# Projection pairs of a two-block layer: a wider allowance for VectorE's side tasks, another order of the projections around the pooling products, and the pooling gate stored and multiplied later

## The chip, the core and the metric

The kernel runs on one core of a Trainium2 chip. The metric is device time in microseconds (us), a median over runs. The engines: PE (matmuls), DVE (VectorE), ACT (ScalarE), POOL (GpSimd) and SP, which here only issues DMAs. Each engine takes its instructions in the order in which the program wrote them, and waits at an instruction until what it needs is there.

## What is computed

Two layers, one after the other, on a sequence of 1024 positions and width 1024, in float32. The change lies in the first one, a layer with three branches:

```
proj = u @ w_in + b_in            # 96 column tiles of 128
a_v, a_g, b_b, b_c, b_h, b_g, c_a, c_b, c_g, merge = jnp.split(proj, ...)
pooled = causal_multiscale_pool(a_v)          # windows 2, 4, 8, 16, four groups
y_a = einsum("bsgi,gio->bsgo", pooled, pool_w) * pool_scale * silu(a_g)
y_b = b_b * causal_dwconv(b_c * b_h, sc_w, sc_b) * silu(b_g)
h_c = causal_dwconv(c_a * sigmoid(c_b), cf_w, cf_b)      # 31 taps
y_c = silu(layer_norm(h_c)) * silu(c_g)
m = sum over n of sigmoid(merge)[n] * (y_n @ w_branch[n])
```

Then come an output projection with a layer norm, and a second layer (attention, gating and a gated MLP).

## The kernel before

Every float32 matmul is made of three products of split operands: a number is split into a high part (a copy rounded by ACT) and a low part (the difference, by DVE); `hilo` (line 163) does it. A tile is 128 channels by 1024 positions.

**Order of the work.** `self.slots` is a list that the Python program goes through once, in `run`; it writes all instructions out. No scheduler runs on the chip: what stands earlier in an engine's list comes first.

**Projections.** The 96 column tiles of `w_in` are made in two ways. The first 30 are plain slots (`slot_u`): 48 matmuls each. Then come pairs (`pair_u`, run by `run_two`): two column tiles together in seven products of 12 matmuls (a scheme that saves one product in eight), into two of four PSUM pairs. Between the products DVE combines PSUM halves (tiles `two` and `pp`), makes weight sums (`sums`) and low parts (`w`, `A`) for this pair and the next; ACT makes the high parts and one copy out of PSUM per pair (`two`, line 451), for which the fourth product waits. The name `raw` is a pair's loaded weights.

**Side tasks of DVE.** The 31-tap convolution is 31 DVE instructions per channel tile: one at line 720 and 30 taps (`h<-p,par_t,h`). They wait in a queue, `bgq`. A plain slot takes `bg` of them. In a pair, `fill` (line 439) takes tasks as long as an account of DVE's time, `now[0]`, stays within 0.2 us of that of the products, `now[1]`; each task has a cost in the account. A pair's epilogue (its activations, stores and DVE steps) is a task list too, done in the next pair. When a convolution tile is done, ACT squares it and POOL adds it and its square to two sums (lines 735, 736).

**Pooling.** `open_a` first takes everything that is left in `bgq` and then changes the SBUF pool. For each of the groups 3, 2, 1, 0 there are then: a pair for `a_v`, a pair for `a_g`, and `pool_slot`, 24 matmuls with the small `pool_w`. The pooled sums (`s`, `v`, `cn`) and their split (`ph`, `pl`) are tasks of the `a_v` pair's epilogue, made by DVE during the `a_g` pair; `split` of the second half comes last. The tile `v` has one buffer. The gates `ag` stay in SBUF, and line 971 multiplies the pooling result by scale and gate in one DVE step before the store to `ya_sp`.

**Branch products.** `end` loads the first branch weights (`wr`) and half of `yb_sp` when the last pooling product is due; `first_y` splits that half, `open_q` loads the rest (`ld`), and `branch` runs the 24 products of the three branches, b first, then a, then c. For branch c `prep_y` normalises and multiplies before it splits.

Of the kernel before, what the change touches and what calls it, by code (L numbers as in the profile page):

```python
# [21 lines left out]
H = 512  # L22
# [83 lines left out]
class Kernel:  # L106
# [125 lines left out]
    def run(self):  # L232
# [45 lines left out]

        self.release, self.resume = release, resume
        self.dma_ahead, self.split_ahead, self.hl = dma_ahead, split_ahead, hl  # L280
# [113 lines left out]
    def run_two(self, g, n):  # L394
# [44 lines left out]
        def fill():  # L439
            while later or self.bgq:  # L440
                q = later or self.bgq
                cost = getattr(q[0], "cost", 1.3)
                if now[0] + cost > now[1] + 0.2:
                    return
                q.popleft()()
                now[0] += cost
# [259 lines left out]
    def block1(self):  # L706
# [3 lines left out]
        d = lambda n, m=NK: [self.dram.tile([P, 1024], F, name="%s%d" % (n, i)) for i in range(m)]  # L710
        h_sp, ya_sp, yb_sp, cg_sp, mg_sp, m_sp = (
            d("h_sp"), d("ya_sp"), d("yb_sp"), d("cg_sp"), d("mg_sp", 24), d("m_sp"))
        st_sp = d("st_sp", 2)
# [138 lines left out]
        for j in range(plain):  # L852
            for ct, epi in ((C_B, epi_cb), (C_A, epi_ca), (B_C, lambda j: short_conv(j)[0]),
                            (B_H, epi_bh), (B_G, lambda j: short_conv(j)[4]), (B_B, epi_bb)):
                if j or ct in (B_H, B_G, B_B):
                    self.slot_u(ct + j, epi(j), bg=5)
                    self.slots[-1].aux = 1 if j > 1 else 0
                    if self.slots[-1].aux:
                        self.slots[-1].bg = 4
        pairs = Pairs(self.pair_tiles(lambda: self.cw, 1, True), lambda: None, lambda: None)  # L860
# [5 lines left out]
        self.slots[-2].tail = lambda: self.two_begin(pairs)  # L866
        self.slots[-1].tail = begin
        self.slots.append(Slot(pre=lambda: self.open_psum(4, 0)))

# [5 lines left out]
        merge = iter(range(0, 24, 2))  # L875
        gate = iter(range(0, 8, 2))

# [23 lines left out]
        def epi_av(g):  # L901
            def one(j, ps):
                s = {}
                c = lambda: self.c1.tile([P, 1040], F, tag="s", name="s", bufs=2)

                def head():
                    v = s["v"] = s["c"] = self.c1.tile([P, 1040], F, tag="v", name="v")
                    s["w"] = 1
                    nc.gpsimd.memset(v[:, 0:16], 0.0)
                    self.act(v[:, 16:1040], ps, AF.Identity, bias=self.bias_in(A_V + j))  # L910
                    if j % 2 == 0:
                        T["pw"] = self.c1.tile([P, H], F, tag="pw", name="pw")
                        nc.sync.dma_start(T["pw"], I["pool_w"][g])

                def double():
                    cur, w = s["c"], s["w"]
                    nxt = c()
# [19 lines left out]
                n = g + 1  # L937
                return [Task(0, head)] + [Task(1.25, double)] * n + [Task(1.8, out), Task(1.25, split)]
# [7 lines left out]
        def epi_ag(g):  # L946
            def one(j, ps):
                t = self.c1.tile([P, 1040], F, tag="s", name="ag", bufs=2)
                T["ag", j] = t[:, 0:1024]
                self.act(T["ag", j], ps, AF.Silu, bias=self.bias_in(A_G + j))  # L950
            return lambda x, y: [Task(0, lambda: one(2 * g, x)), Task(0, lambda: one(2 * g + 1, y))]

        def pool_slot(g):
            s = {}

            def mm():
# [11 lines left out]
            def one(c):  # L968
                j = 2 * g + c
                e = T["ag", j]  # L970
                self.stt(e, s["ps"][c], self.par("pool_scale", j), e, ALU.mult, ALU.mult)
                nc.sync.dma_start(ya_sp[j], e)

            def epi():
                pairs.todo = [Task(1.3, lambda: one(0)), Task(1.3, lambda: one(1))]
                if g == 0:
                    first_y()
                    pairs.flush()

            self.slots.append(Slot([], mm, epi, pre=pairs.flush, name="pool%d" % g))  # L980

        def open_a():
# [5 lines left out]
            self.ca = ExitStack()  # L988
            self.c1 = self.ca.enter_context(self.pool("ca", reuse_waits="tile"))

        self.slots.append(Slot(pre=open_a))
        for g in (3, 2, 1, 0):
            pair_u(A_V + 2 * g, A_V + 2 * g + 1, epi_av(g))
            pair_u(A_G + 2 * g, A_G + 2 * g + 1, epi_ag(g))
            pool_slot(g)

        def end():
# [4 lines left out]
            for j in range(4):  # L1002
# [4 lines left out]
                nc.sync.dma_start(T["ld"][1, j], yb_sp[j])  # L1007

        def last_pool():
            pairs.flush()  # L1010
            end()
            self.split_ahead(1)

        self.slots[-1].pre = last_pool

# [13 lines left out]
        def load_y(n, j):  # L1029
            if j < 8 and (n, j) not in T["ld"]:  # L1030
                t = T["ld"][n, j] = self.c1.tile([P, 1024], F, tag="ld", name="ld", bufs=4)
                nc.sync.dma_start(t, {0: ya_sp, 1: yb_sp, 2: h_sp}[n][j])
                if n == 2:
                    t = T["ld"]["cg", j] = self.c1.tile([P, 1024], F, tag="ld", name="ld", bufs=4)
                    nc.sync.dma_start(t, cg_sp[j])

        def open_q():
            self.ca.close()
            cwx.close()
            self.ca = ExitStack()  # L1040
            self.c1 = self.ca.enter_context(self.pool("cq", reuse_waits="tile"))
            for j in range(4, 8):
                load_y(1, j)
            T["g"], T["mi"] = {}, {}
            load_g(1, 0)
            for j in range(4, 8):
# [3 lines left out]
            self.rs_h = self.c1.tile([P, 1024], F, name="rs_h")  # L1050
            T["cb"] = self.c1.tile([P, 1024], F, name="cb2")
            nc.sync.dma_start(self.mu_h, st_sp[0])
# [4 lines left out]
        def load_g(n, d):  # L1057
            if d < 8:
                T["g"][n, d] = self.c1.tile([P, 1024], F, tag="g", name="g", bufs=3)
# [26 lines left out]
        def prep_y(n, j):  # L1086
            load_y(n, j)
            load_y(n, j + 1)
            if n == 2:
                t, e = T["ld"][2, j], T["ld"].pop(("cg", j))  # L1090
                self.tt(t, t, self.mu_h, ALU.subtract)
                self.tt(t, t, self.rs_h, ALU.mult)
                self.act(t, t, AF.Silu, scale=self.par("cf_g", j), bias=self.par("cf_be", j))
                self.tt(t, t, e, ALU.mult)
            split_y(n, j)

        def branch(n, d, bg):
            s = {}

            def pre():  # L1100
# [3 lines left out]
                elif n == 1:  # L1104
                    for j in (2 * d - 8, 2 * d - 7):
                        load_y(0, j)
                        self.bgq.append(lambda j=j: split_y(0, j))
                elif n == 0:
# [723 lines left out]
    def pair_tiles(self, pool, raws, e_right=False):  # L1832
# [3 lines left out]
        def tile(which, n):  # L1836
            if which in ("a", "b", "c", "e"):
                if not kept:
                    p, = self.open_right("wab")
                    w = [p.tile([P, 1024], R, name="w%d" % i) for i in range(5)]  # L1840
                    kept.update(a=w[:2], b=(self.A1[:, 9216:10240], w[2]), c=w[3:], e=p)
                if which == "e":
# [259 lines left out]
```

## Time and profile before

| what | us |
|---|---|
| median of 3 runs (2826.72 to 2831.49) | 2829.41 |
| the profiled execution, its own time | 2825.78 |
| span in its trace | 2823.9 |
| PE busy | 2657.8 |
| DVE busy | 1825.3 |
| ACT busy | 944.4 |
| POOL busy | 140.5 |

The prediction reads the page (busy time by engine, and the span in 40 slices), the waits (who waited for whom), timelines (instructions in order of time: start, duration, engine, line, operation, and in brackets the engine's idle time before it and what ended it), stretches (busy time per engine in a window), and the DMA list (bytes, and the time from issue to landing). Equal instructions that follow each other stand in one row with a count.

### The profile page before, as it was taken

The numbers are of one execution on the slowest core, as the hardware profiler recorded it, in microseconds if no ns is written. First come the engines' busy times: TensorE is split into PE (matmuls) and PEld (weight loads), VectorE is DVE, ScalarE is ACT, GpSimd is POOL, SyncE is SP. The second block draws the span as 40 slices with busy tenths as digits, with TensorE's granted clock in tenths as the row PEclk, the third lists the DMA queues.
The fourth block names the chain that finished last, engine by engine and source line by source line (L and its number), as shares of the span: only waits on it lengthen the run. The fifth ranks groups of instructions, "written<-read, shape, count | busy, mean of one in ns | idle before, by whom it ended". The sixth has DMA issues, their size and how long they took to land.

```text
span 2823.9 us, 29288 instructions
## 1 busy us (share of the span) xinstructions
PE 2657.8 (94%) x11820; PEld 2177.3 (77%) x11820; DVE 1825.3 (65%) x2007; ACT 944.4 (33%) x1202; POOL 140.5 (5%) x131
## 2 busy tenths in 40 slices
PE   5999999999994688899999999999999999999999
PEld 3888878878783466688878788888888788887887
DVE  6787888787879655547466245545747688884343
ACT  6312233334331222323234245542323334432222
POOL 4000000000000000000014010000000000000000
PEclk9999999999997799999999999999999999999999
DMA  5111212313121111667542222212432221214554
GB/s 224 55 65 60 75 65 78 120 68 112 71 108 52 71 49 54 238 249 279 179 156 90 69 83 75 75 34 87 158 136 90 75 90 68 90 67 138 175 170 159
DMA packets 90570, 307.59 MB, mean 109 GB/s; under 512 B 10177, under 2 KB 10689, under 8 KB 90434
## 3 DMA queue, kind: packets, MB, share of 16 engines
q1 hardware_dynamic: 90434, 305.71, 30.3%
q8 instruction: 93, 1.52, 0.2%
q14 instruction: 43, 0.35, 0.0%
HBM read 234.37 MB, written 71.30 MB: 108 GB/s over the span
## 4 chain that ended last, share of the span: by engine, by line
PE 52%; DVE 3%; DMA 2%; ACT 1%; issue 1%; POOL 0%; SPq 0%; DVEq 0%; ACTq 0%; POOLq 0%
PE pp L142 50%; PE pm L142 1%; PE pp L145 1%; DVE z L161 1%; DVE wl L158 0%; ACT oj L155 0%; PE pm L145 0%; DMA wr<-in_w_out 0%; DVE A L158 0%; DMA adag<-in_ada 0%; DVE B L158 0%; ACT B L164 0%; POOL ox L1279 0%; ACT wh L164 0%; DVE ox L158 0%
## 5 line engine op out<-in xcount | busy, mean ns | idle before, releaser
L142 PE MATMUL pp<-A,wh 128*128 128x512 f32 x2432 | 769.3, 392 | 12.9 <-DVE A L158 8.3
L142 PEld LDWEIGHTS pp<-A,wh 128*128 128x128 f32 x2432 | 454.5, 188 | 114.1 <-DVE A L158 9.9
L142 PE MATMUL pp<-A,wl 128*128 128x512 f32 x1296 | 505.9, 390 | 1.2 <-DVE wl L158 1.2
L142 PE MATMUL pp<-A,w 128*128 128x512 f32 x1664 | 443.9, 392 | 64.6 <-ACT two L451 55.4
L142 PE MATMUL pp<-B,A 128*128 128x512 f32 x1676 | 487.8, 391 | 1.2 <-DVE B L158 1.1
L158 DVE TENSOR_TENSOR wl<-wr,wh 128x1024 fp32r<-128x1024 f32 (+1 forms) x164 | 197.0, 1202 | 344.7 <-ACT wh L164 341.5
L142 PEld LDWEIGHTS pp<-A,w 128*128 128x128 f32 x1664 | 314.6, 189 | 133.0 <-ACT two L451 56.2
L142 PE MATMUL pp<-B,w 128*128 128x512 f32 x1136 | 380.1, 394 | 10.8 <-DVE two L158 10.8
L142 PEld LDWEIGHTS pp<-B,A 128*128 128x128 f32 x1676 | 314.3, 188 | 67.9 <-DVE B L158 2.3
L161 DVE SCALAR_TENSOR_TENSOR h<-p,par_t,h 128x1024 f32<-128x1024 f32 x240 | 313.9, 1308 | 4.7
L142 PEld LDWEIGHTS pp<-A,wl 128*128 128x128 f32 x1296 | 243.8, 188 | 53.3 <-DVE wl L158 2.5
L164 ACT CAST wh<-wr 128x1024 fp32r<-128x1024 f32 (+1 forms) x164 | 164.8, 1006 | 345.9 <-PE pp L142 324.2
L142 PE MATMUL pp<-B,wh 128*128 128x512 f32 x800 | 262.0, 393 | 9.2 <-DVE ag L161 7.0
L142 PEld LDWEIGHTS pp<-B,w 128*128 128x128 f32 x1136 | 216.6, 191 | 57.5 <-DVE two L158 12.1
L142 PEld LDWEIGHTS pp<-B,wh 128*128 128x128 f32 x800 | 150.6, 189 | 42.2 <-issue 7.8
L372 ACT CAST w<-raw 128x1024 fp32r<-128x1024 f32 x50 | 52.7, 1054 | 272.6 <-PE pp L142 177.7
L142 PE MATMUL pp<-wh,gh 128*128 128x512 f32 x352 | 138.1, 392 | 4.7 <-ACT gh L164 4.7
L142 PE MATMUL pp<-wl,gh 128*128 128x512 f32 x352 | 137.9, 392 | 0.3 <-DVE wl L158 0.3
L142 PE MATMUL pp<-wh,gl 128*128 128x512 f32 x352 | 137.8, 391 | 0.1
L158 DVE TENSOR_TENSOR two<-pp,two 128x512 f32<-128x512 f32 x100 | 68.8, 689 | 99.8 <-PE pp L142 99.3
L142 PE MATMUL pp<-A,A 128*128 128x512 f32 x324 | 126.8, 391 | 0.4 <-DVE A L158 0.3
L142 PE MATMUL pp<-B,wl 128*128 128x512 f32 x320 | 125.3, 392 | 0.0
(256 smaller groups left out, 3016.3 us busy)
## 6 DMA issues: line engine op xcount, KB each, us to landing
raw<-in_w_in SPq DMA_DIRECT2D x66, 512.0 KB, 3.7
wr<-in_w_in SPq DMA_DIRECT2D x63, 512.0 KB, 3.5
wr<-in_w_dn SPq DMA_DIRECT2D x44, 512.0 KB, 3.6
raw<-in_w_up SPq DMA_DIRECT2D x34, 512.0 KB, 5.2
mg_sp<-e SPq DMA_DIRECT2D x24, 512.0 KB, 2.9
wr<-in_w_br SPq DMA_DIRECT2D x24, 512.0 KB, 5.9
g<-mg_sp SPq DMA_DIRECT2D x24, 512.0 KB, 5.9
g_sp<-z SPq DMA_DIRECT2D x22, 512.0 KB, 3.0
```

The source lines that it names most:

```text
L142: return self.nc.tensor.matmul(*a, **k)
L145: self.nc.tensor.transpose(*a)
L158: return self.nc.vector.tensor_tensor(out, a, b, op)
L161: self.nc.vector.scalar_tensor_tensor(out, a, s, b, op0, op1)
L164: self.nc.scalar.copy(hi, src)
L372: self.nc.scalar.copy(t.__dict__[which][0], src)
```

## The change

1. In the plain slots `bg` was 5 (4 from the third channel tile on). Now it is 6 for the first two channel tiles, and 3, 6, 4 or 5 by kind of slot after that; the last plain slot takes none, and the account starts the pairs with `late = 3.0`.
2. `fill` lets a task end up to 1.0 us past the products' account, instead of 0.2. This holds for the second layer's MLP pairs too.
3. Four of the twelve merge pairs move from before `open_a` to between the pooling products. Each `a_v` pair is now followed by two pairs before its pooling product. The second half of the pooling chain goes into `bgq`, and what is left of it is taken just before the product.
4. The gate `a_g` is stored to `ag_sp` like the other gates. The pooling result leaves PSUM through ACT (scale only). From `open_a` on, the tiles `e`, through which these stores go, have one buffer (`n_e = 1`). Branch a loads both and multiplies in `prep_y`.
5. Two weight buffers of the pairs swap places for an odd split count, and `open_q` issues its loads in another order and fetches two merge gates early.

```diff
@@ run_two / fill
-                if now[0] + cost > now[1] + 0.2:
+                if now[0] + cost > now[1] + 1.0:
@@ block1
-                    self.slot_u(ct + j, epi(j), bg=5)
+                    self.slot_u(ct + j, epi(j), bg=6 if j < 2 else {B_H: 3, B_G: 6, B_B: 4}.get(ct, 5))
                     self.slots[-1].aux = 1 if j > 1 else 0
-                    if self.slots[-1].aux:
-                        self.slots[-1].bg = 4
...
+        self.slots[-1].bg = 0
+        pairs.late = 3.0
...
-        for what in "M G C5 B5 M M G M C6 M B6 M G M M C7 B7 M G M M M".split():
+        for what in "M G C5 B5 M M G C6 M B6 M G M C7 B7 M G M".split():
...
-            return lambda x, y: one(2 * g, x) + [Task(0.7, wsplit)] + one(2 * g + 1, y)
...
+            def epi(x, y):
+                a, b = one(2 * g, x), one(2 * g + 1, y)
+                late = b[1:] + [Task(0.7, wsplit)]
+                return [Task(0, wload)] + a + [b[0], Task(0, lambda: self.bgq.extend(late))]
...
+            def pre():
+                while self.bgq:
+                    self.bgq.popleft()()
+                pairs.flush()
+                if g == 0:
+                    end()
+                    self.split_ahead(1)
...
             def one(c):
-                j = 2 * g + c
-                e = T["ag", j]
-                self.stt(e, s["ps"][c], self.par("pool_scale", j), e, ALU.mult, ALU.mult)
-                nc.sync.dma_start(ya_sp[j], e)
+                e = e_tile()
+                self.act(e, s["ps"][c], AF.Identity, scale=self.par("pool_scale", 2 * g + c))
+                nc.sync.dma_start(ya_sp[2 * g + c], e)
...
+            self.n_e = 1
...
-        for g in (3, 2, 1, 0):
+        for g, rest in ((3, "AA"), (2, "AM"), (1, "AM"), (0, "MM")):
             pair_u(A_V + 2 * g, A_V + 2 * g + 1, epi_av(g))
-            pair_u(A_G + 2 * g, A_G + 2 * g + 1, epi_ag(g))
+            for what in rest:
+                if what == "M":
+                    add_merge()
+                else:
+                    i = next(pool_gate)
+                    pair_u(A_G + i, A_G + i + 1, epi_store(A_G + i, AF.Silu, ag_sp, i))
             pool_slot(g)
...
@@ prep_y
+            t, e = T["ld"][n, j], T["ld"].pop(("g", n, j))
             if n == 2:
-                t, e = T["ld"][2, j], T["ld"].pop(("cg", j))
...
-                self.tt(t, t, e, ALU.mult)
+            self.tt(t, t, e, ALU.mult)
```

**Place 1, DVE at `open_a`.** The rows of DVE in the program's order, before: the end of the last pair ahead of the pooling pairs, then what `open_a` takes out of the queue, then the first pooling pair. `h<-p` is a tap, line 720 begins a new channel tile, `w<-sums` is the first step of the next pair.

```order
L158 TENSOR_TENSOR w_2357<-raw,w_2356 128x1024
L158 TENSOR_TENSOR pp<-pp,two 128x512
L158 TENSOR_TENSOR w_2358<-sums,A_193 128x1024
L158 TENSOR_TENSOR A_193<-raw,A_193 128x512
L158 TENSOR_TENSOR pp<-pp,two 128x512
L161 SCALAR_TENSOR_TENSOR h<-p,par_t,h 128x1024 x8
L720 TENSOR_SCALAR h<-p,par_t 128x1024
L161 SCALAR_TENSOR_TENSOR h<-p,par_t,h 128x1024 x30
L158 TENSOR_TENSOR w_2360<-sums,w_2359 128x1024
```

The same place now:

```order
L158 TENSOR_TENSOR w_2391<-raw,w_2390 128x1024
L158 TENSOR_TENSOR pp<-pp,two 128x512
L158 TENSOR_TENSOR w_2393<-sums,A_201 128x1024
L158 TENSOR_TENSOR A_201<-raw,A_201 128x512
L158 TENSOR_TENSOR pp<-pp,two 128x512
L161 SCALAR_TENSOR_TENSOR h<-p,par_t,h 128x1024 x5
L158 TENSOR_TENSOR w_2394<-sums,w_2392 128x1024
```

Where 38 taps and a new tile's first step stood, 5 taps stand; the others moved to earlier slots and pairs.

**Place 2, ACT around the first pooling product (group 3).** Before, from the last step of the `a_v` epilogue (`ph`, the pooled high part) over the two gates `ag` to the high part `w` and the PSUM copy `two` of the next pair:

```order
L164 CAST ph<-v 128x1024
L155 ACT_TABLE_LOAD
L155 ACTIVATE ag<-pp,par_t 128x1024 x2
L372 CAST w_2359<-sums 128x1024
L451 COPY two<-pp 128x512
```

Now, from the last high parts before the pooling product. The first `e` row is the two gates, the second the two pooling results.

```order
L164 CAST ph<-v 128x1024
L372 CAST A_201<-raw 128x512
L164 CAST pwr<-pw 128x512
L155 ACTIVATE e<-pp,par_t 128x1024 x2
L372 CAST w_2392<-sums 128x1024
L155 ACTIVATE e<-pp,par_t 128x1024 x2
L451 COPY two<-pp 128x512
```

The next pair's copy `two` now stands behind four activations that share one buffer, and so behind the landing of three stores.

**Place 3, SP after the last pooling pair.** Before: the weights of the branch products (`wr`), half of `yb_sp`, then the stores of the last pooling results and the loads of the other half.

```order
L246 DMA wr<-in_w_br 128x1024 x2
L1007 DMA raw<-yb_sp_99 128x1024
L1007 DMA raw<-yb_sp_100 128x1024
L1007 DMA sums<-yb_sp_101 128x1024
L1007 DMA sums<-yb_sp_102 128x1024
L246 DMA wr<-in_w_br 128x1024 x2
L972 DMA ya_sp_91<-ag 128x1024
L972 DMA ya_sp_92<-ag 128x1024
L1032 DMA ld<-yb_sp_103 128x1024
```

Now:

```order
L831 DMA mg_sp_145<-e 128x1024
L831 DMA mg_sp_146<-e 128x1024
L246 DMA wr<-in_w_br 128x1024 x2
L1018 DMA raw<-yb_sp_99 128x1024
L1018 DMA raw<-yb_sp_100 128x1024
L1018 DMA sums<-yb_sp_101 128x1024
L1018 DMA sums<-yb_sp_102 128x1024
L246 DMA wr<-in_w_br 128x1024 x2
L977 DMA ya_sp_91<-e 128x1024
L977 DMA ya_sp_92<-e 128x1024
L1068 DMA g<-mg_sp_131 128x1024
L1036 DMA ld<-yb_sp_103 128x1024
```

The loads `wr` now stand behind the stores of the last merge pair, and a load of a merge gate stands ahead of `ld`; the rest of the order is as it was.

More of the change, by code (lines that the diff above doesn't have):

```diff
@@ L277, in resume @@
             self.limit = held.pop(0)
-        self.release, self.resume = release, resume
+        self.release, self.resume, self.n_split = release, resume, lambda: st["split"]
         self.dma_ahead, self.split_ahead, self.hl = dma_ahead, split_ahead, hl
@@ L710, in block1 @@
         d = lambda n, m=NK: [self.dram.tile([P, 1024], F, name="%s%d" % (n, i)) for i in range(m)]
-        h_sp, ya_sp, yb_sp, cg_sp, mg_sp, m_sp = (
-            d("h_sp"), d("ya_sp"), d("yb_sp"), d("cg_sp"), d("mg_sp", 24), d("m_sp"))
+        h_sp, ya_sp, yb_sp, ag_sp, cg_sp, mg_sp, m_sp = (
+            d("h_sp"), d("ya_sp"), d("yb_sp"), d("ag_sp"), d("cg_sp"), d("mg_sp", 24), d("m_sp"))
         st_sp = d("st_sp", 2)
@@ L875, in block1 @@
         merge = iter(range(0, 24, 2))
-        gate = iter(range(0, 8, 2))
+        gate, pool_gate = iter(range(0, 8, 2)), iter(range(0, 8, 2))
         def add_merge():
@@ L903, in one @@
                 s = {}
-                c = lambda: self.c1.tile([P, 1040], F, tag="s", name="s", bufs=2)
                 def head():
@@ L910, in head @@
                     self.act(v[:, 16:1040], ps, AF.Identity, bias=self.bias_in(A_V + j))
-                    if j % 2 == 0:
-                        T["pw"] = self.c1.tile([P, H], F, tag="pw", name="pw")
-                        nc.sync.dma_start(T["pw"], I["pool_w"][g])
                 def double():
                     cur, w = s["c"], s["w"]
-                    nxt = c()
+                    nxt = self.c1.tile([P, 1040], F, tag="s", name="s", bufs=2)
                     lo = 2 * w - 1
@@ L935, in split, with wload @@
                     T["pool", j] = (ph, pl)
-                n = g + 1
-                return [Task(0, head)] + [Task(1.25, double)] * n + [Task(1.8, out), Task(1.25, split)]
+                return [Task(0, head)] + [Task(1.25, double)] * (g + 1) + [
+                    Task(1.8, out), Task(1.25, split)]
+            def wload():
+                T["pw"] = self.c1.tile([P, H], F, tag="pw", name="pw")
+                nc.sync.dma_start(T["pw"], I["pool_w"][g])
             def wsplit():
@@ L942, in wsplit @@
                 self.hilo(*T["pwr"], T["pw"])
-            return lambda x, y: one(2 * g, x) + [Task(0.7, wsplit)] + one(2 * g + 1, y)
[L946 to L951, printed above, removed]
+            def epi(x, y):
+                a, b = one(2 * g, x), one(2 * g + 1, y)
+                late = b[1:] + [Task(0.7, wsplit)]
+                return [Task(0, wload)] + a + [b[0], Task(0, lambda: self.bgq.extend(late))]
+            return epi
         def pool_slot(g):
             s = {}
+            def pre():
[5 more added lines that the diff above has]
+                    self.split_ahead(1)
             def mm():
@@ L968, in one @@
             def one(c):
-                j = 2 * g + c
-                e = T["ag", j]
-                self.stt(e, s["ps"][c], self.par("pool_scale", j), e, ALU.mult, ALU.mult)
-                nc.sync.dma_start(ya_sp[j], e)
+                e = e_tile()
+                self.act(e, s["ps"][c], AF.Identity, scale=self.par("pool_scale", 2 * g + c))
+                nc.sync.dma_start(ya_sp[2 * g + c], e)
             def epi():
-                pairs.todo = [Task(1.3, lambda: one(0)), Task(1.3, lambda: one(1))]
+                pairs.todo = [Task(0, lambda c=c: one(c)) for c in range(2)]
                 if g == 0:
@@ L978, in epi @@
                     pairs.flush()
-            self.slots.append(Slot([], mm, epi, pre=pairs.flush, name="pool%d" % g))
+            self.slots.append(Slot([], mm, epi, pre=pre, name="pool%d" % g))
         def open_a():
@@ L1007, in end @@
                 nc.sync.dma_start(T["ld"][1, j], yb_sp[j])
[L1009 to L1014, printed above, removed]
         def open_y(n):
@@ L1032, in load_y @@
                 nc.sync.dma_start(t, {0: ya_sp, 1: yb_sp, 2: h_sp}[n][j])
-                if n == 2:
-                    t = T["ld"]["cg", j] = self.c1.tile([P, 1024], F, tag="ld", name="ld", bufs=4)
-                    nc.sync.dma_start(t, cg_sp[j])
+                if n != 1:
+                    t = T["ld"]["g", n, j] = self.c1.tile([P, 1024], F, tag="ld", name="ld", bufs=4)
+                    nc.sync.dma_start(t, (cg_sp if n else ag_sp)[j])
         def open_q():
@@ L1041, in open_q @@
             self.c1 = self.ca.enter_context(self.pool("cq", reuse_waits="tile"))
+            T["g"], T["mi"] = {}, {}
+            load_g(1, 0)
+            T["g"][1, 1] = self.c1.tile([P, 1024], F, tag="g", name="g", bufs=3)
+            T["g"][1, 2] = self.c1.tile([P, 1024], F, tag="g", name="g", bufs=3)
+            T["cb"] = self.c1.tile([P, 1024], F, name="cb2")
             for j in range(4, 8):
                 load_y(1, j)
-            T["g"], T["mi"] = {}, {}
-            load_g(1, 0)
+            for j in (1, 2):
+                nc.sync.dma_start(T["g"][1, j], mg_sp[8 + j])
             for j in range(4, 8):
@@ L1050, in open_q @@
             self.rs_h = self.c1.tile([P, 1024], F, name="rs_h")
-            T["cb"] = self.c1.tile([P, 1024], F, name="cb2")
             nc.sync.dma_start(self.mu_h, st_sp[0])
@@ L1057, in load_g @@
         def load_g(n, d):
-            if d < 8:
+            if d < 8 and (n, d) not in T["g"]:
                 T["g"][n, d] = self.c1.tile([P, 1024], F, tag="g", name="g", bufs=3)
@@ L1106, in pre @@
                         load_y(0, j)
[L1107 removed]
+                        self.bgq.append(lambda j=j: prep_y(0, j))
                 elif n == 0:
@@ L1840, in tile @@
                     w = [p.tile([P, 1024], R, name="w%d" % i) for i in range(5)]
+                    if self.n_split() % 2:
+                        w[2], w[3] = w[3], w[2]
                     kept.update(a=w[:2], b=(self.A1[:, 9216:10240], w[2]), c=w[3:], e=p)
```

## The prediction

> **What bounds the kernel now.** The page comes first: the busy time of each engine, and PE in the 40 slices of the span.
>
> ```profile
> PE 2657.8 (94%) x11820; PEld 2177.3 (77%) x11820; DVE 1825.3 (65%) x2007; ACT 944.4 (33%) x1202; POOL 140.5 (5%) x131
> ...
> PE   5999999999994688899999999999999999999999
> ```
>
> PE is the bound, and the change removes no matmul: it can only take away time in which PE waits or runs slowly. Apart from the start, that time lies in one place, slices 13 to 17, around 850 to 1200 us. The waits of PE say for whom:
>
> ```profile
> PE pp L142 <- ACT two L451: 55.4, 2, 54.7
> PE pp L142 <- ACT ph L164: 20.5, 4, 7.9
> PE pp L142 <- ACT pwr L164: 14.6, 3, 5.7
> PE pp L142 <- DVE two L158: 10.8, 3, 3.9
> PE pp L142 <- DVE ag L161: 10.3, 4, 7.0
> ```
>
> One wait of 54.7 us, about 35 us ahead of pooling products (`ph`, `pwr`), and small ones. The timeline of PE shows an undisturbed pair and the long wait:
>
> ```profile
> 839.93 2.88 PE L142 MATMUL pp<-A,w 128*128 128x512 f32 x12
> 858.97 2.88 PE L142 MATMUL pp<-A,w 128*128 128x512 f32 x12
> 867.13 5.60 PE L142 MATMUL pp<-A,w 128*128 128x512 f32 x24
> 932.85 5.38 PE L142 MATMUL pp<-A,w 128*128 128x512 f32 x12 [54.68 <-ACT two L451]
> ...
> 1154.34 0.39 PE L142 MATMUL pp<-ph,pwr 128*128 128x512 f32 x1
> ```
>
> The same product returns after 858.97 − 839.93 = 19.04 us: a pair of 84 matmuls without a wait, 2.72 a product, 0.227 a matmul. The row at 867.13 holds the last product of the last pair before `open_a` and the first of the next, which starts at 869.85. The last pooling matmul starts at 1154.34 and is done at about 1154.6. In these 284.7 us lie 8 pairs (152.3) and 4 pooling products of 24 matmuls (5.44 each): 174.1 us. So 110.6 us are lost. The long wait takes 54.68, and the 12 matmuls behind it ran 5.38 instead of 2.88: 57.2. The other 53.4 belong to pooling. The timeline of DVE and ACT tells why PE waited:
>
> ```profile
> 870.65 10.52 DVE L161 SCALAR_TENSOR_TENSOR h<-p,par_t,h 128x1024 f32<-128x1024 f32 x8
> 881.94 43.51 DVE L161 SCALAR_TENSOR_TENSOR h<-p,par_t,h 128x1024 f32<-128x1024 f32 x30
> ...
> 925.53 1.06 ACT L155 ACTIVATE e<-h 128x1024 f32<-128x1024 f32 x1 [43.21 <-DVE h L161]
> 930.26 1.11 ACT L155 ACTIVATE e<-pp,par_t 128x1024 f32<-128x1024 f32 x1 [2.68 <-POOL hq L736]
> 932.21 0.59 ACT L451 COPY two<-pp 128x512 f32<-128x512 f32 x1
> ```
>
> DVE emptied its queue, 38 taps in a row; ACT stood at the square of the finished tile, and behind it in ACT's order was the copy that PE's fourth product needs.
>
> **The convolution pairs: −12.3 us.** Before pooling, PE's small losses are these:
>
> ```profile
> 376.00:859.00 483.00, 471.03 (x2055) 387.98 (x2054) 392.06 (x410) 169.12 (x182) 15.90 (x12) 0.99 0.26 95
> ...
> 391.20 4.60 PE L142 MATMUL pp<-B,w 128*128 128x512 f32 x12 [3.94 <-DVE two L158]
> 588.08 3.01 PE L142 MATMUL pp<-B,w 128*128 128x512 f32 x12 [3.57 <-DVE two L158]
> 744.78 5.49 PE L142 MATMUL pp<-B,w 128*128 128x512 f32 x12 [3.30 <-DVE two L158]
> ```
>
> 483 − 471.03 = 12.0 idle, and 1.7 + 2.6 in the slow rows at 391 and 744: 16.3. The first wait came of six taps ahead of DVE's first steps for a pair; by the new order none stands there. The other two came where `epi_ca` took taps out of a queue longer than 32; the new order has no run of taps there. In their place DVE gets fuller. It was busy 392.06 us over 25.4 pairs (483 / 19.04), 15.4 each, with 96 taps. Now, by the order, 110 taps lie in 21 pairs, 1.45 more each, at 10.52 / 8 = 1.32 us: 1.9 more, and 0.2 as the b and c steps fall on fewer pairs. That is 17.5 of 19.04: still covered on average. Where a tile ends it can be short:
>
> ```profile
> 867.93 1.22 DVE L158 TENSOR_TENSOR w<-sums,A 128x1024 fp32r<-128x1024 f32 x1
> ...
> 739.51 3.42 DVE L158 TENSOR_TENSOR w<-sums,w 128x1024 fp32r<-128x1024 f32 x1
> ...
> 738.99 2.85 POOL L736 TENSOR_TENSOR hq<-hq,e 128x1024 f32<-128x1024 f32 x1
> ```
>
> A DVE step of 1.22 us took 3.42 beside a POOL addition. With DVE some 1 us behind by the new allowance, and 2.72 us from the fifth product's end until its combined half is needed, I count 1.3 us for each of three tile ends: 4 (bounds 0 and 10). The Trainium skill, GPSIMD Engine Reference, section Specifications, says that the SBUF interfaces are shared with VectorE and that DVE instructions with two SBUF inputs contend. The row agrees; if by that rule the two POOL steps held DVE up whole (about 5.3 us a tile), this term would be some 8 us larger.
>
> **The flush: −48.1 us.** Five taps are left: 5 × 1.32 = 6.6, begun 0.8 after the pair's end (870.65 against 869.85), so 7.4. From the last tap's end (925.45) to the copy's (932.80) it took 7.35, and this chain (square, POOL's two additions, the second `e`, a high part) stays; a table load that joins lies inside the wait for POOL. The copy is done at 14.75, and three products take 8.16: PE waits 6.6, plus 2.5 for the slow product, 9.1 instead of 57.2. What is late next is the same chain, no longer the taps. Bounds 6 and 13.
>
> **The pooling products: −47.4 us.** Before, PE stood while the second half's chain ran:
>
> ```profile
> 978.70 0.80 PE L142 MATMUL pp<-ph,pwr 128*128 128x512 f32 x1 [7.92 <-ACT ph L164]
> 1006.04 2.99 PE L142 MATMUL pp<-A,w 128*128 128x512 f32 x12 [1.09 <-DVE ag L161]
> ```
>
> Now each chain has two pairs (38 us) to hide in, and by the order all of it but `pwr` (group 3) stands in them. DVE's multiplication by the gate goes too, and so the 1.09. What comes in their place is the single buffer `e`, whose price is a store's landing:
>
> ```profile
> mg_sp<-e SPq DMA_DIRECT2D x22, 512.0 KB, 2.9
> ...
> mg_sp<-e SPq DMA_DIRECT2D x4, 512.0 KB, 4.6
> ...
> cb<-in_c SPq DMA_DIRECT2D x1, 512.0 KB, 10.0
> ```
>
> The first row is the convolution pairs' stores, the others are from 840 to 1200 us. No run of two `e` that wait for a landing is in this trace; I take 2.9 with 0.1 for the hand-over, as raw loads run beside it there as here. After a pooling product the copy `two` stands behind four `e` of 1.1 and three landings: 0.7 + 4.4 + 9.0 + 0.6 = 14.7 us from the pair's end, against 5.44 + 8.16 = 13.6 of PE's work: 1.1 us, three times. In group 3, `pwr` adds about 2 us. In four pairs one landing stands ahead of the copy (about 8.3 against 8.16): 0.7 together. Sum 6 instead of 53.4; bounds 2 and 30 (15 landings at 4.6 make 25 more).
>
> **After the last pooling product: +9 us.** Here the change adds a wait.
>
> ```profile
> 1161.78 1.19 PE L142 MATMUL pp<-B,wh 128*128 128x512 f32 x2 [7.05 <-DVE ag L161]
> 1169.72 0.49 PE L142 MATMUL pp<-B,wh 128*128 128x512 f32 x1
> ...
> 1168.62 1.05 ACT L164 CAST B<-ld 128x1024 fp32r<-128x1024 f32 x1 [10.39 <-DMA ld<-yb_sp]
> ...
> 1139.25 0.81 SPq L246 DMA_DIRECT2D wr<-in_w_br  x2
> 1163.28 2.29 SPq L1032 DMA_DIRECT2D ld<-yb_sp  x4
> ...
> sums<-yb_sp SPq DMA_DIRECT2D x2, 512.0 KB, 7.9
> ```
>
> SP issued `wr` at 1139, well before the pooling product ended (1154.6). Now SP first waits for the last merge pair's two stores: 0.7 + 1.1 + 3.0 + 1.1 = 5.9 us after the pair's end. Queued behind on SP are `wr`, `raw`, `sums`, which ACT's splits wait for, and behind those stands ACT's first pooling `e`, which frees the PSUM that PE needs. Six loads take about 10 us (1.9 to the last issue, estimated from the rows' spacing, and 7.9): 16.3, two copies and `e` 2.2: 18.5. PE's product ends at 5.4, so it waits 13 instead of 7.2: +5.9. Then `ld` waits for the second pooling `e` (18.5 + 3.0 + 1.1 = 22.6), and lands 0.4 + 5.3 later (1168.62 − 1163.28) with 2.4 for the split: 30.8. PE needs it 7.9 after its start (1169.72 − 1161.78), at 26.4: 4.4 instead of about 1.6. Bounds 3 and 16.
>
> **What costs nothing.**
>
> ```profile
> 284.00:355.00 71.00, 71.00 (x315) 58.80 (x314) 58.15 (x48) 17.70 (x15) 5.27 (x4) 1.00 0.21 70
> ...
> 1207.00:1278.00 71.00, 71.00 (x315) 58.80 (x314) 32.53 (x30) 16.95 (x16) 0.00 (x0) 1.00 0.68 246
> 1278.00:1349.00 71.00, 71.00 (x315) 58.80 (x314) 53.50 (x47) 21.86 (x21) 0.00 (x0) 1.00 0.79 294
> ```
>
> In the plain slots at most one more tap falls on 10.9 us (48 matmuls): 58.15 + 6.5 × 1.32 = 66.7 of 71 us, and the weights' split stands ahead of the taps; PE stays covered (0 to 4 if not). Branch a's eight multiplications of 1.22 lie in a stretch where DVE is busy 32.5 of 71 us. Its eight loads of 512 KB put 96 GB/s on top of 246 for 44 us, 0.95 of the DMA engines' time if the share grows in step; 0 to 6, taken as 0. The MLP pairs get the same 1.0 us; PE's slices are full there, so nothing is to be had, and the task that runs over ends inside the 2.72 us of the next product. The buffers' swap frees DVE, not PE. The two merge gates fetched early only come earlier.
>
> **Sum.** −12.3 − 48.1 − 47.4 + 9 = −98.8. The profiled execution had 2825.78 us, the median is 3.6 above it; on the median's scale 2829.41 − 98.8 = **2731 us**. About 0.2% (5.7 us) can be told from no change.
>
> **The rivals.**
> - *DVE becomes the bound in the convolution pairs.* For it: 17.5 of 19.04, before waits on ACT and POOL; taps at 43.51 / 30 = 1.45 add 0.7 a pair. Against it: the account charges more than DVE takes (1.25 for a step of 1.22). 21 × 0.7 = 15: 2746. Chance 0.13.
> - *Stores land at 4.6.* Fifteen landings stand ahead of a copy or load that PE needs (9, 4 and 2): 15 × 1.7 = 25: 2756. Against it: those four stores had a flush's traffic around them. 0.17.
> - *Each small wait costs clock.* Behind a wait of 3.30 twelve matmuls took 5.49, behind 3.57 only 3.01, behind 1.09 2.99: nothing between is shown. If all eight new waits cost 2.6: +21, 2752. By the Trainium skill, TensorE: Matmul & The Clock Gate, section What's actually happening, half rate returns only after an idle window of about 3.4 us, so these waits would be free; the row at 744.78 came in under that. 0.07.
> - *Slower: landings as long as the longest row, 10.0.* 15 × 7.1 = 107, more than the gain: 2838. It decides from 2.9 + 98.8 / 15 = 9.5 us a landing. Against it: 2.9 in 22 stores. 0.02.
> - *The flush stays,* because DVE reaches it late. Against it: 5 taps by the order; 30 us of lag would be needed to lose half the term, about 2761. 0.02.
>
> My forecast has 0.59. With all four terms at their low bounds (−4, −3, −4, −6) it comes to 2714, with half of the sum of the high bounds' excess that lies outside the rivals (+6, +4, +7, halved) to 2740. The range adds the spread of the runs (about 2.5 to either side) and reaches over the first three rivals, 2756 being the highest, with some of a second one on top: 2710 to 2764. Faster 0.97, the same 0.01, slower 0.02.
>
> **What would show it.** Right: no wait of PE above 8 us between 850 and 1100 us; five taps before the first pooling pair; `ph` gone from PE's waits; the wait before the first branch product about 13 us. Wrong: PE waiting for `two` by more than 3 us in the pairs behind pooling products (landings), many waits for `two` or `pp` before 800 us (DVE), PE waits between 1180 and 1350 us of the new span (DMA).

## The result and the profile after

The changed kernel takes 2746.61 us (median of 3 runs, 2743.31 to 2748.19) against 2829.41: a ratio of 0.9706 (95% interval 0.9684 to 0.9728), 82.8 us less. The forecast was 2731, in a range of 2710 to 2764: the side and the range hold, and the gain is some 16 us smaller than forecast. The two profiled executions lie 79.2 us apart (2825.78 and 2746.61).

The page of the changed kernel, busy times and PE's 40 slices:

```profile
PE 2650.9 (97%) x11820; PEld 2172.8 (79%) x11820; DVE 1817.7 (66%) x2007; ACT 961.4 (35%) x1214; POOL 142.2 (5%) x131
...
PE   5999999999999997999999999999999999999999
```

The hole of slices 13 to 17 is closed; one slice (1030 to 1100 us) still shows a 7. PE's waits, total, count and longest:

```profile
PE pp L142 <- ACT two L451: 13.8, 6, 6.5
PE pp L142 <- ACT e L155: 13.7, 1, 13.7
...
PE pp L142 <- ACT B L164: 5.5, 2, 4.7
```

`ph` is gone, and `two` has fallen from 55.4 to 13.8. PE's timeline, rows with a wait; the first two lie in the convolution pairs, the others from `open_a` on:

```profile
483.79 3.04 PE L142 MATMUL pp<-B,w 128*128 128x512 f32 x12 [1.16 <-DVE two L158]
491.29 5.74 PE L142 MATMUL pp<-A,w 128*128 128x512 f32 x24 [1.36 <-DVE pp L158]
...
798.61 5.49 PE L142 MATMUL pp<-A,w 128*128 128x512 f32 x12 [6.46 <-ACT two L451]
...
852.62 0.73 PE L142 MATMUL pp<-ph,pwr 128*128 128x512 f32 x2 [1.56 <-DVE pwr L158]
...
868.86 4.61 PE L142 MATMUL pp<-A,w 128*128 128x512 f32 x12 [2.76 <-ACT two L451]
...
935.24 3.03 PE L142 MATMUL pp<-A,w 128*128 128x512 f32 x12 [1.85 <-ACT two L451]
...
1000.79 3.01 PE L142 MATMUL pp<-A,w 128*128 128x512 f32 x12 [1.68 <-ACT two L451]
...
1070.82 1.22 PE L142 MATMUL pp<-B,wh 128*128 128x512 f32 x2 [13.71 <-ACT e L155]
...
1082.64 0.80 PE L142 MATMUL pp<-B,wh 128*128 128x512 f32 x1 [4.66 <-ACT B L164]
...
1269.43 0.50 PE L142 MATMUL pp<-B,wh 128*128 128x512 f32 x1 [0.89 <-ACT B L164]
1270.69 0.50 PE L142 MATMUL pp<-B,wh 128*128 128x512 f32 x1 [0.76 <-DVE B L158]
```

Most stand nearly as forecast: 6.46 (forecast 6.6), 1.56 (2), 13.71 (13), 4.66 (4.4). To find the rest I cut PE's time into five places, at the same matmul in each kernel. The windows of the changed kernel (length, then PE busy and, behind it, the number of matmuls; the third number from the end is PE's granted clock):

```profile
374.17:791.05 416.88, 411.74 (x1804) 337.69 (x1803) 380.85 (x392) 146.68 (x156) 18.35 (x10) 1.00 0.26 92
791.27:814.04 22.77, 16.30 (x60) 12.91 (x59) 9.89 (x12) 10.38 (x11) 4.77 (x3) 0.85 0.33 124
814.26:1056.70 242.44, 233.24 (x1011) 190.04 (x1010) 150.94 (x190) 89.16 (x97) 0.78 (x7) 0.99 0.25 93
1056.92:1101.38 44.46, 25.63 (x95) 20.09 (x95) 17.08 (x16) 16.32 (x16) 0.00 (x0) 0.77 0.76 291
...
1109.26:1358.56 249.30, 245.85 (x1080) 202.28 (x1079) 144.82 (x143) 58.05 (x55) 1.65 (x1) 0.99 0.64 231
```

They are the convolution pairs, `open_a`, pooling, the first branch product, and the other branch products. What a place loses is its length less 2.72 / 12 for each matmul. A window starts 0.20 us behind a matmul's start and ends 0.02 ahead of one's, so that none counts twice, and these 0.22 are added: 416.88 + 0.22 − 1804 × 0.22667 = 8.2. For the last place the loss is what it takes above the kernel before, where PE stood nowhere (242.76 us). The same cut of the kernel before:

```profile
374.60:877.08 502.48, 490.51 (x2140) 404.10 (x2139) 407.61 (x426) 171.75 (x185) 15.90 (x12) 0.99 0.26 94
877.30:948.07 70.77, 16.09 (x60) 12.75 (x59) 56.88 (x46) 10.04 (x11) 10.81 (x5) 0.61 0.12 48
948.29:1154.32 206.03, 165.51 (x675) 130.26 (x674) 122.00 (x149) 55.31 (x62) 0.78 (x7) 0.90 0.18 65
1154.54:1186.77 32.23, 24.42 (x95) 19.34 (x95) 18.04 (x18) 9.88 (x10) 0.00 (x0) 0.89 0.74 270
...
1194.65:1437.41 242.76, 242.76 (x1080) 201.30 (x1079) 135.73 (x135) 58.51 (x55) 1.65 (x1) 1.00 0.61 220
```

| us lost by PE | before | forecast of the gain | after | gain | missing |
|---|---|---|---|---|---|
| convolution pairs | 17.6 | 12.3 | 8.2 | 9.4 | 2.9 |
| `open_a` | 57.4 | 48.1 | 9.4 | 48.0 | 0.1 |
| pooling | 53.2 | 47.4 | 13.5 | 39.7 | 7.7 |
| behind the last pooling product | 10.9 | −9 | 23.1 | −12.2 | 3.2 |
| the other branch products | 0 | 0 | 6.5 | −6.5 | 6.5 |

The gains sum to 78.4 of the 79.2; the plain slots and all behind the branches move by less than 1 us together. So the question is what makes up the 20 us in the last column, and which edit won what.

### The profile page after: what moved, and what is told of

Its sections match the earlier page's. It is cut to its first block, busy times and chain, and to the rows that moved or that the text cites. A ratio compares the mean times of both kernels' runs of the same rounds, so it can differ in the third digit from the quotient of the medians.

```text
span 2744.8 us, 29345 instructions
## 1 busy us (share of the span) xinstructions
PE 2650.9 (97%) x11820; PEld 2172.8 (79%) x11820; DVE 1817.7 (66%) x2007; ACT 961.4 (35%) x1214; POOL 142.2 (5%) x131
## 4 chain that ended last, share of the span: by engine, by line
PE 75%; DVE 11%; DMA 5%; ACT 4%; issue 3%; SPq 1%; POOL 1%; DVEq 0%; ACTq 0%; POOLq 0%
PE pp L142 73%; DVE h L161 2%; DVE sums L158 1%; ACT e L155 1%; DMA ld<-ag_sp 1%; DVE wl L158 1%; DVE A L158 1%; DVE ld L158 1%; PE pm L142 1%; DVE pp L158 1%; DVE g L158 1%; DMA ld<-h_sp 1%; DVE w L158 1%; PE pp L145 1%; PE pm L145 1%
## 5 line engine op out<-in xcount | busy, mean ns | idle before, releaser
L142 PEld LDWEIGHTS pp<-A,wh 128*128 128x128 f32 x2432 | 454.6, 188 | 115.3 <-DVE A L158 10.9
L142 PE MATMUL pp<-A,w 128*128 128x512 f32 x1664 | 446.6, 395 | 23.1 <-ACT two L451 13.8
L161 DVE SCALAR_TENSOR_TENSOR z<-pp,par_t,z 128x1023 f32<-128x1023 f32 x88 | 112.6, 1280 | 52.3 <-ACT z L155 51.3
```

The source lines that it names most:

```text
L142: return self.nc.tensor.matmul(*a, **k)
L161: self.nc.vector.scalar_tensor_tensor(out, a, s, b, op0, op1)
```

## The experiments

My theory was that each place has its own cause: store landings in pooling, a chain of loads in the branches, and that the account and the order of the pairs win what the forecast gave them. Rivals stand with each run.

**The account alone.** The kernel before with the allowance, the plain slots' numbers and the buffers' swap, and without the other edits:

```diff
-                if now[0] + cost > now[1] + 0.2:
+                if now[0] + cost > now[1] + 1.0:
...
+        self.slots[-1].bg = 0
+        pairs.late = 3.0
...
+                    if self.n_split() % 2:
+                        w[2], w[3] = w[3], w[2]
```

> The kernel before with the account alone: the 1.0 us by which a task may end past a step, the plain slots' new numbers of tasks, the late allowance of 3.0 and the swap of the two weight buffers. The order of the pairs, the gate's multiplication and the pooling stay as before. By the order no tap is left for open_a (25 pairs instead of 21 take them). My account by place: the convolution pairs lose 8 us instead of 17.5, the wait at open_a falls from 57.3 to 0 to 3, pooling (53.0) and the wait behind it (10.9) stay: 64 to 67 less than before, 2763 us (2759 to 2769). Rival 1, DVE is the bound with 1.45 more taps in a pair: 0.7 us in each of 25 pairs, about 2783 us, with many waits of PE for two and pp. Rival 2, the flush goes only because pairs were moved away from ahead of it: about 2819 us.

Measured: 2747.76 us, a ratio of 0.9715 (0.9701 to 0.9730), 15 us better than expected and level with the whole change. None of the three times expected came, neither mine nor a rival's. Its windows, cut as above:

```profile
374.54:867.64 493.10, 488.14 (x2140) 400.55 (x2139) 427.91 (x442) 177.15 (x190) 23.57 (x13) 1.00 0.28 101
867.86:881.24 13.38, 13.38 (x60) 11.08 (x59) 8.16 (x10) 4.40 (x5) 0.00 (x0) 1.00 0.07 18
881.46:1076.97 195.51, 164.18 (x675) 130.04 (x674) 121.13 (x149) 55.24 (x62) 0.78 (x7) 0.91 0.18 63
1077.19:1108.67 31.48, 24.35 (x95) 19.62 (x95) 18.12 (x18) 10.24 (x10) 0.00 (x0) 0.84 0.79 300
...
1116.54:1359.29 242.75, 242.75 (x1080) 201.30 (x1079) 135.98 (x135) 58.51 (x55) 1.66 (x1) 1.00 0.62 220
```

The losses are 8.2, 0, 42.7, 10.2 and 0. The pairs and `open_a` came as expected. Pooling fell too, from 53.2 to 42.7, which I had not seen: the allowance holds for pooling's tasks as well. PE's waits in this run show where:

```profile
PE pp L142 <- ACT ph L164: 19.8, 3, 7.4
...
PE pp L142 <- ACT pwr L164: 6.3, 2, 3.2
```

`pwr` stood at 14.6 before: 8.3 of the 10.5 us are the weights' split, which now comes earlier. In group 3 it is done inside the pair, and its wait of 3.16 is gone; in groups 2 and 1 the waits fell from 5.70 and 5.71 to 3.16 each. That the allowance does this, and not another of the four edits, was not tried apart. Against this run the rest of the change (moved pairs, stored gate) wins 42.7 − 13.5 = 29.2 in pooling, and gives back 9.4 at `open_a` (four pairs fewer to take taps), 12.9 behind the last product and 6.5 in the branches: 0.4 us remain.

**The old allowance, with all else changed.** `+ 1.0` back to `+ 0.2` in the changed kernel.

> The changed kernel with the old allowance of 0.2 us; all else as changed. By the order 46 taps and a first step are left when open_a comes. If DVE's chain alone sets that wait: 0.8 + 46 x 1.32 + 0.8 + 7.35 for the square, POOL and copy, less three products of 8.16, and 2.5 of slow clock behind it: 64 us instead of 9.4, so 55 more than the changed kernel, 2801 us (2795 to 2808); the pooling stage and the branches stay as changed. Rival, the taps are not what the time hangs on (the gain of the changed kernel came with the order of the pairs): no more than 10 us above the changed kernel, 2757 us.

Measured: 2803.03 us (ratio 0.9910, 0.9896 to 0.9925). The `open_a` window of this run:

```profile
788.97:870.15 81.18, 15.93 (x60) 12.64 (x59) 67.16 (x54) 11.44 (x12) 10.81 (x5) 0.60 0.11 41
```

The loss is 67.8 (64 expected). The two edits are not additive: without the allowance the moved pairs make the flush longer, with it they only bring back 9.4. The other half of that expectation did not hold. Cut in the same way, pooling loses 17.8 here instead of 13.5 (one wait of 6.67 for `pwr`), and the convolution pairs 5.2 instead of 8.2: the wider allowance costs PE 3 us there.

**The branches: load or multiplication?** Two kernels: without the gate's load, the piece multiplied by itself (first diff), and with the load but not multiplied (second).

```diff
-                if n != 1:
+                if n == 2:
                     t = T["ld"]["g", n, j] = self.c1.tile([P, 1024], F, tag="ld", name="ld", bufs=4)
...
-            t, e = T["ld"][n, j], T["ld"].pop(("g", n, j))
+            t = T["ld"][n, j]
+            e = T["ld"].pop(("g", n, j)) if n else t
```

> The changed kernel without branch a's load of its stored gate: the pooled tile is multiplied by itself instead, so the output of branch a is left wrong and eight DVE multiplications stay. In the changed kernel PE loses 1.4, 1.2 and 3.8 us at three places between 1178 and 1275 us, where the kernel before loses nothing. If the loads are the cause (two tiles for each piece in a ring of four buffers, so a piece waits for its landing): all three go, about 6 us less, 2740 us. If the longer chain on DVE and ACT is (the multiplication has to be done ahead of ACT's split): the three stay, 2746 us.

```diff
-            self.tt(t, t, e, ALU.mult)
+            if n:
+                self.tt(t, t, e, ALU.mult)
```

> The changed kernel with the gate loaded for branch a, but not multiplied (eight DVE operations of 1.22 us are left out, and the gate from the result). If the loads are the cause of the 6.4 us that PE loses between 1178 and 1275 us: they stay within 2 us, 2745 us. If the chain on DVE and ACT is: they go, 2740 us.

Measured: 2738.61 and 2739.37 us (ratios 0.9686, 0.9670 to 0.9702, and 0.9688, 0.9674 to 0.9702). The last window of each:

```profile
1107.49:1350.25 242.76, 242.76 (x1080) 201.37 (x1079) 144.72 (x143) 58.27 (x55) 1.65 (x1) 1.00 0.62 220
```

```profile
1107.06:1349.81 242.75, 242.75 (x1080) 201.37 (x1079) 134.06 (x131) 58.38 (x55) 1.66 (x1) 1.00 0.65 235
```

Both take the loss away whole, so it is not the one or the other, as I had set it up. Load and multiplication are links of one chain: a tile of the ring is free again only when the piece is loaded, multiplied and split. DVE in the changed kernel, and the landings of the ring's tiles:

```profile
1176.51 1.22 DVE L158 TENSOR_TENSOR ld<-ld 128x1024 f32<-128x1024 f32 x1 [2.06 <-DMA ld<-ag_sp]
1178.85 1.22 DVE L158 TENSOR_TENSOR A<-ld,A 128x1024 fp32r<-128x1024 f32 x1 [1.11 <-ACT A L164]
...
DMA to landing us min/median/max: 4.2/6.8/8.9
```

The piece's split ended at 1180.07, and PE, which had waited for it 0.76 us, went on at 1180.13. With one link less the chain has slack. That the ring's four buffers are the limit is the reading that fits both runs; a deeper ring was not tried.

**The changed kernel a second time.**

> The changed kernel unaltered, a second time. Its profile lost 6.4 us between 1178 and 1275 us, where the run with the small allowance, with the same order of instructions there, lost 0.2. If the eight pieces of branch a form a chain through a ring of four buffers, whose landings of 4.2 to 8.9 us add up and leave no slack, the loss there comes out anywhere from 0 to 7 us, while every other place repeats within 1 us; the median lies between 2741 and 2748. Rival, the loss follows from the order of the instructions alone: 6.4 us again, within 1.

Measured: 2743.13 us (ratio 0.9703, 0.9688 to 0.9717). The 0.2 in that expectation was miscounted: the run with the small allowance had two more waits at 1326 to 1328 us, and lost 2.7 in the branches. The windows from pooling on of the second run:

```profile
814.55:1056.62 242.07, 232.89 (x1011) 190.09 (x1010) 151.09 (x190) 89.21 (x97) 0.79 (x7) 0.99 0.25 92
1056.84:1101.16 44.32, 25.62 (x95) 20.12 (x95) 17.03 (x16) 16.33 (x16) 0.00 (x0) 0.77 0.78 294
...
1109.02:1355.94 246.92, 243.94 (x1080) 201.07 (x1079) 144.26 (x142) 58.05 (x55) 1.66 (x1) 1.00 0.64 233
```

Pooling 13.1 and 23.0 behind it repeat within 0.4; the branches lose 4.2 instead of 6.5. Over the five profiles that share this order in the branches it is 2.7, 3.7, 4.2, 6.5 and 6.6: a chain at its limit, not a fixed cost. PE's idle time in it is only 1.7 to 3.5 us; the rest, 1.0 to 3.1, are matmuls that took longer behind the waits.

**No waits for landings near pooling.**

```diff
-                e = e_tile()
+                e = self.c1.tile([P, 1040], F, tag="s", name="ye", bufs=2)[:, 0:1024]
                 self.act(e, s["ps"][c], AF.Identity, scale=self.par("pool_scale", 2 * g + c))
```

and the second tile of the pair ahead of a pooling product goes into `v` in the same way.

> The changed kernel with other buffers for what ACT writes near pooling: both scaled pooling tiles go into the two buffers s, which are idle by then, and the second tile of the pair ahead of each pooling product goes into the idle buffer v, so no tile waits for the landing of the one before it. If the landings are what PE waits for behind pooling products: the losses of 4.6, 2.1 and 1.9 us there fall to 0.5 or less each, 8 us; behind the last product the loads come 2.8 us earlier and those of the second half 3.7 more, so 23.1 becomes about 16. Together 15 less, 2731 us (2727 to 2737). Rival, ACT's own work (four tiles of 1.1 us, splits) sets these waits: no more than 3 us less, 2743 us or above.

Measured: 2730.35 us (ratio 0.9659, 0.9644 to 0.9673). Pooling and what is behind it:

```profile
814.92:1051.31 236.39, 231.96 (x1011) 190.36 (x1010) 151.43 (x190) 89.14 (x97) 0.79 (x7) 0.99 0.26 97
1051.53:1088.82 37.29, 24.52 (x95) 19.37 (x95) 17.08 (x16) 15.77 (x15) 0.00 (x0) 0.82 0.82 318
```

Losses of 7.4 and 16.0, against 13.5 and 23.1. The three waits behind pooling products (2.76, 1.85 and 1.68) are gone, so landings were their cause, and ACT's own work was not. Behind the last product the second wait fell from 4.66 to 0.86, but the first only from 13.71 to 11.14: most of that one has another cause. In pooling 6 instead of 8 us were won: a wait for `two` in the last group, 0.61 us in the changed kernel, was 2.29 here, and took 4.2 with its slow clock.

**Branch a's pieces spread out.** One piece in each of the first branch's products; the gate's dot products go to the third branch:

```diff
-                if n == 1 and d < 4:
-                    gate_dot(2 * d)
-                    gate_dot(2 * d + 1)
-                elif n == 1:
-                    for j in (2 * d - 8, 2 * d - 7):
-                        load_y(0, j)
-                        self.bgq.append(lambda j=j: prep_y(0, j))
+                if n == 2:
+                    gate_dot(d)
+                elif n == 1:
+                    load_y(0, d)
+                    self.bgq.append(lambda: prep_y(0, d))
```

> The changed kernel with branch a's eight pieces prepared one in each of the first branch's eight products, instead of two in each of the last four; the dot products of the out gate, which stood in the first four, move to the third branch. If the loss of 6.4 us comes of a chain of loads without slack: it goes and does not come back in the third branch, 0 to 6 us less than the changed kernel, 2741 us at the median. Rival, eight more loads in this stretch are too much for the DMA engines wherever they are put: PE still loses 3 us or more between the first branch and the out phase.

Measured: 2738.05 us (ratio 0.9690, 0.9675 to 0.9704), with the branches at 242.75 us, undisturbed. The eight loads and multiplications cost PE nothing where the chain has time, and the DMA engines are not the limit here.

**Together.** Both edits, and the branch loads issued ahead of the last stores (`end()` ahead of `pairs.flush()`), and ACT's last pooling tiles ahead of its splits (`first_y()` behind `pairs.flush()`).

> The two edits before together, and two more: the loads for the branches are issued ahead of the last pair's stores, and ACT scales the last pooling tiles ahead of its splits of the loaded ones. Pooling 8 to 9 us less, branches 0 to 6 less. Behind the last pooling product PE needs split weights, one loaded piece and a free PSUM tile: loads from about 1051 us, landed by 1057 to 1061, split by 1064, so PE waits 6 to 7 us instead of 13.7, and 1 to 2 for the second half instead of 5: 11 instead of 23. Together 23 to 27 less than the changed kernel, 2721 us (2715 to 2728). Rival, the loads share the DMA engines with the stores that they are moved ahead of, and nothing is won at that place: 2732 us or above.

Measured: 2721.57 us (ratio 0.9630, 0.9614 to 0.9646). PE behind the last pooling product:

```profile
1051.54 0.49 PE L142 MATMUL pp<-B,wh 128*128 128x512 f32 x1 [2.35 <-ACT B L164]
...
1066.10 0.80 PE L142 MATMUL pp<-B,wh 128*128 128x512 f32 x1 [6.20 <-ACT B L164]
```

The first wait was 13.71 in the changed kernel and 11.14 without the landing waits; here it is 2.35, below the expected 6 to 7. So the order on SP and ACT was its main cause; which of the two moves did more was not tried. The second half's loads became the limit (6.20 instead of 1 to 2), and the place loses 14.0 instead of 23.1.

**One merge pair back ahead of `open_a`,** in the changed kernel and in the one called together:

```diff
-        for what in "M G C5 B5 M M G C6 M B6 M G M C7 B7 M G M".split():
+        for what in "M G C5 B5 M M G C6 M B6 M G M C7 B7 M G M M".split():
...
-        for g, rest in ((3, "AA"), (2, "AM"), (1, "AM"), (0, "MM")):
+        for g, rest in ((3, "AA"), (2, "AM"), (1, "AM"), (0, "M")):
```

> The changed kernel with one merge pair moved back from the last pooling group to the place ahead of open_a: 22 pairs take taps, and by the order the last of them stands in the 22nd, none at open_a. If the loss of 9.0 to 9.5 us at open_a comes of the five taps and the chain behind them, it falls to 0 to 1, and group 0's second half still hides in its one remaining pair (one doubling, some 7 us of chain in 19 us): 8.5 us less than the changed kernel, 2736 us (2731 to 2741; the branches' loss varies by some 6 from run to run). Rival, the last group needs both pairs: PE waits 3 us or more for ph or pl at its product, or more behind it, and the time stays at 2743 us or above.

> The kernel of the run called together, with the same merge pair moved back ahead of open_a. Its losses there were 7.9 in the convolution pairs, 9.0 at open_a, 5.3 in pooling, 14.0 behind the last product. With the taps gone from open_a: 8.5 less, 2713 us (2709 to 2718). Rival, group 0's second half does not fit its one pair, and the gain comes back as a wait for ph: 2720 us or above.

Measured: 2738.06 us (ratio 0.9675, 0.9659 to 0.9691) and 2714.41 us (0.9592, 0.9578 to 0.9607). The windows of the second, the fastest kernel of this study:

```profile
374.89:811.38 436.49, 431.00 (x1888) 353.31 (x1887) 396.43 (x406) 158.91 (x169) 24.21 (x13) 1.00 0.27 99
811.60:824.98 13.38, 13.38 (x60) 11.08 (x59) 8.16 (x10) 4.40 (x5) 0.00 (x0) 1.00 0.08 22
825.20:1039.13 213.93, 211.31 (x927) 173.42 (x926) 142.82 (x180) 84.94 (x93) 0.79 (x7) 1.00 0.28 101
1039.35:1075.26 35.91, 28.17 (x95) 21.84 (x95) 15.65 (x14) 14.01 (x14) 0.00 (x0) 0.81 0.86 334
...
1082.20:1324.96 242.76, 242.76 (x1080) 201.30 (x1079) 143.91 (x146) 56.41 (x53) 1.66 (x1) 1.00 0.64 233
```

The places lose 8.8, 0, 4.0, 14.6 and 0, against 8.2, 9.0, 5.7, 14.0 and 0 in the run called together. In the first of the two kernels they lose 8.9, 0, 13.4, 23.8 and 6.6, against 8.2, 9.4, 13.5, 23.1 and 6.5. The loss at `open_a` goes and comes back nowhere; the last group needs one pair only.

## Why the prediction was right, and where not

**Right: what bounds the kernel, and the flush.** Every gain lies where PE stood before. The flush term came out at 48.0 of 48.1, with the chain it named, and the run with the old allowance, expected by the same working, came within 4 us.

**Right in the sum, silent on whose gain it is.** The steps went place by place through the whole change and never asked which edit wins what. When I did ask, in the expectation for the account alone, I gave pooling to the order of the pairs, and that was wrong. The account's edits alone give the whole time. They take all 57.4 at `open_a` and 10.5 in pooling; the moved pairs and the stored gate pay elsewhere for what they win. The 9 us that the prediction left at `open_a` are the price of the moved pairs: I counted the five taps left, and not that they were left because four pairs had gone.

**Pooling: the mechanism right, the size too small.** "1.1 us, three times" was 2.76, 1.85 and 1.68. ACT after the pooling product of group 2:

```profile
920.54 1.28 ACT L155 ACT_TABLE_LOAD   x1 [3.09 <-DVE pp L158]
921.84 1.12 ACT L155 ACTIVATE e<-pp,par_t 128x1024 f32<-128x1024 f32 x1
925.87 1.12 ACT L155 ACTIVATE e<-pp,par_t 128x1024 f32<-128x1024 f32 x1 [2.91 <-DMA mg_sp<-e]
...
929.72 1.12 ACT L155 ACTIVATE e<-pp,par_t 128x1024 f32<-128x1024 f32 x1 [1.80 <-DMA mg_sp<-e]
933.60 1.11 ACT L155 ACTIVATE e<-pp,par_t 128x1024 f32<-128x1024 f32 x1 [2.77 <-DMA ya_sp<-e]
934.61 0.58 ACT L451 COPY two<-pp 128x512 f32<-128x512 f32 x1
...
859.51 1.12 ACT L155 ACTIVATE e<-pp,par_t 128x1024 f32<-128x1024 f32 x1 [6.34 <-DMA ag_sp<-e]
```

The four tiles and three landings are as forecast, 2.7 to 2.9 from the end of one tile to the next (the wait of 1.80 is the rest of one, behind a split of 1.04). A table load of 1.28 stands ahead of them that I had placed in a wait at `open_a` only. In group 3 (the last row) one landing took 6.34, behind two weight loads that SP had just issued. And the first product behind it ran slowly: 4.61 instead of 2.88. The longer waits (3.0) and this product (1.7) make 4.7 of the missing 7.7; the rest lies in smaller waits and in the matmuls behind them. "Stores land at 4.6" as a general rule, the rival, did not come: the median of the stores into `ag_sp` and `ya_sp` is 2.9 and 2.6.

**Behind the last product: both waits nearly right, the clock left out.** The waits came at 13.71 and 4.66 (13 and 4.4). Of the missing 3.2 us, 1.7 are the matmuls behind the second wait, which the forecast let run at full speed: PE's granted clock was 0.54 in the 5.4 us from 1082.6 on, and 1.00 at the same place before. The matmuls behind the first wait ran 0.8 faster than before. The rest comes from the waits themselves: the first rose by 6.7 instead of 5.9, and the second half's, from 0.76 to 4.66 and 0.46, by 4.4 instead of 2.8.

**The branches: the step "branch a's multiplications and loads, taken as 0" failed.** It looked at shares (DVE 32.5 of 71 us, DMA 0.95) and not at the chain of one piece through a ring of four buffers. Its upper bound of 6 for the loads is close to the loss of 6.5, but that bound came from the DMA engines' share, which was not the cause.

**The convolution pairs:** 8.2 left instead of 4. PE's idle time is 5.1 us, in seven waits of 0.21 to 1.36. Four of them (3.9 us) come during POOL's additions at the first two tile ends (467 to 473 and 573 to 581 us) or within 18 us behind them; the third tile end, at 680 to 685, has none, and the other three waits lie near no tile end. So the place that the forecast named fits in part only. With the old allowance the pairs lost 5.2. The rival that DVE becomes the bound is not borne out (15 were its price).

**"Each small wait costs clock"** did not decide, but it is not empty. In the fastest kernel four waits behind the last pooling product, 7.7 us together, were followed by matmuls that took 6.9 us longer than without a wait (granted clock 0.81 in this window). The last section shows more.

**The signs.** `ph` is gone and five taps stand before the first pooling pair. But "no wait of PE above 8 us between 850 and 1100 us" could not have held beside the forecast itself: the wait of about 13 us that it asks for ended at 1070.82. Of the signs of being wrong one came clearly, the waits between 1180 and 1350 us, and it marked the step that failed.

## What to carry to other kernels

When a change has several parts, cost each one alone as well as all together: here the edits to a planner's account alone gave the whole gain, and the rest moved losses from one place to three others. Work that is put between two dependent steps hides a wait only there; count what it hid in the place that it leaves. A busy share of half says nothing on a chain of loads through a small ring of buffers: add up one piece's way through the ring, and compare it with the time that the consumer gives it.

## What the runs showed of the hardware

PE's clock behind a wait follows no length that these runs could fix. The second run of the changed kernel, and the run with the small allowance:

```profile
867.92 4.61 PE L142 MATMUL pp<-A,w 128*128 128x512 f32 x12 [1.81 <-ACT two L451]
```

```profile
1061.20 4.61 PE L142 MATMUL pp<-A,w 128*128 128x512 f32 x12 [1.85 <-ACT two L451]
```

After a wait of 1.85 twelve matmuls took 4.61 here, and 3.03 in the changed kernel at 935.24; after one of 3.57 in the kernel before, 3.01. The granted clock was 0.50 in the slow stretch (869.9 to 871.4 us of the second run) and 1.00 behind the waits that cost nothing. Even two shorter waits can do it: behind 0.89 and 0.76 in the changed kernel the clock was 0.76 over 7 us, and behind 0.93 and 0.77 at the same place in its second run it was 1.00. The Trainium skill, TensorE: Matmul & The Clock Gate, section What's actually happening, lets half rate return only after an idle window of about 3.4 us. The trace does not agree: waits of 1.81 and 1.85 have done it here. What decides was not tried.
